# Two hand-ordered boundaries in a macaron decoder block: earlier transposes, a low half written by hand, and weight splits moved

## The chip, the core and the metric

The kernel runs on one core of a Trainium2 chip. The metric is the device time of one execution in microseconds. Engines are named TensorE (PE in the rows; PEld are its weight loads), VectorE (DVE), ScalarE (ACT), GpSimd (POOL) and SyncE (SP, which issues most transfers).

## The reference

One decoder block over 512 tokens of 1024 channels in float32: a SwiGLU feed-forward (width 2816), a token mixer and a second SwiGLU feed-forward, each between two RMS norms:

```python
f = swiglu(rms_norm(h, ffn1_pre_g), ffn1_w_gu, ffn1_w_down)
h = h + 0.5 * rms_norm(f, ffn1_post_g)
m = hybrid_mixer(rms_norm(h, mix_pre_g), ...)   # one input projection; RG-LRU and window attention; output projection
h = h + rms_norm(m, mix_post_g)
f = swiglu(rms_norm(h, ffn2_pre_g), ffn2_w_gu, ffn2_w_down)
h = h + 0.5 * rms_norm(f, ffn2_post_g)
```

## The kernel before

**Products.** Every float32 operand is split in two halves, a rounded one (`h`) and the rest (`l`), and a product is three matmuls (`mm3`, L166 to L169): high by high, high by low, low by high. The weights come in pieces of 128x1024, numbered in the order of use (`worder`): SP loads a piece (`wload`), ScalarE casts it to its high half (`wround`, L115), VectorE subtracts that from the piece (`wsplit`, L123) and issues the loads of the next three. `wget` takes the next piece and prepares two more ahead; `wnow` prepares none ahead. Pieces 50 to 53 are the mixer's first four x chunks, 54 and 55 its keys, 56 and 57 its values; 124 to 131 are the first gate and up chunks of the second feed-forward.

**The stages.** The first feed-forward's down product is a sum of seven products of blocks in Strassen's manner (order 1, 2, 3, 6, 5, 7, 4 in `down`); the token output projection (`token_out`) is the same in small. The last product, 4, is done for one of its two token tiles after the other: 33 matmuls each in `down` (six pieces, the last of half size), 12 in `token_out`.

**A boundary** between two stages handles four tiles of 128 tokens each (`boundary`). `half(t, i, z)` squares one half of a tile's columns on ScalarE with a sum (L515); `epilogue(t)` is a generator of five steps: (1) the sum and its power on GpSimd, and the gain (L519, L529, L212); (2) the residual sum in two halves on VectorE (L543), its squares on ScalarE (L548) and the store; (3) sum and power of these (L529, L212); (4) the normalised tile `un` in two halves (L556), which yields the number `FEATURE_LAG[name][t]`; (5) `to_features`: eight TensorE transposes (L227), the high half cast on ScalarE (L231), the low half on VectorE (L232), and in the second boundary copies of the raw values on ScalarE (L235). Tiles 0 and 1 are ready before the last product, 2 and 3 after its first and second pass. Boundary `b1` lies between the first feed-forward and the mixer, `b2` between the mixer and the second feed-forward, `b3` at the end.

**Ticks.** A generator that has yielded a number waits in the list `live`; each call of `tick()` lowers the number by one, and at zero the generator's next step is emitted there. In the last product of `down` there is a tick after each weight piece (six to a pass), in the feature chunks one after each chunk.

**Order.** Inside `with tc.manual_schedule()` each engine issues its instructions in the order in which they are written; the order across engines is left to semaphores. Outside of it a planner chooses the order with durations of its own, and it may put instructions written outside between those written inside. In the kernel before, `down` is inside to the end of its last product and of the epilogues that it starts; the mixer, from its first x chunk (`x_group`, `first_four`) on, is outside; `token_out` and the second feed-forward's gate and up stage are inside.

**The next stage's first chunks** need `u`, the transposed tiles: the low token half (tokens 0 to 255) needs tiles 0 and 1, the high half tiles 2 and 3. So the first four x chunks (`first_four`) and the first six chunks of the second feed-forward (`first_six`) are done for the low half first, 24 matmuls of 256 columns each, and then for the high half. The first chunk takes the low parts of `u` last (`low_last`).

Of the kernel before, what the change touches and what calls it, by code (L numbers as in the profile page):

```python
# [18 lines left out]
ATT_LAG = (3, 2)  # L19
WARM = 10  # L20
JSTD = {"f1": 6, "f2": 4}
FEATURE_LAG = {"b1": (7, 9, 7, 3), "b2": (1, 1, 5, 6)}
ATT_GATES = (2, 3, 4, 5, 6, 7)
T = 512
NT = T // P
# [16 lines left out]
def hybrid_block_kernel(ctx, tc, x, xt, g1, w_first, gains, gu1, gs1, dn1, w_x, w_gate, w_q, w_k, w_v, w_gl, w_ga, w_pl, w_pa,  # L42
# [85 lines left out]
    def wget():  # L128
        i = wpos[0]
        wpos[0] += 1  # L130
        wsplit(i + 1 + AHEAD)
        return wready[i]
# [101 lines left out]
                keep.append((raw[half][:, :, ts_], bv))  # L234
        return [lambda z=z, bv=bv: A.copy(z, bv) for z, bv in keep]  # L235

    def feat_chunk(b, w, u, tok, low_last=False):
        wh, wl = w
        if low_last:
            for n in range(2 * KD):  # L240
                k = n % KD
                ks = slice(k * P, (k + 1) * P)
                if n < KD:
                    PE.matmul(b[:, tok], lhsT=wh[:, ks], rhs=at(u, 0, k, tok), start=k == 0, stop=False)
                    PE.matmul(b[:, tok], lhsT=wl[:, ks], rhs=at(u, 0, k, tok), start=False, stop=False)
                else:
                    PE.matmul(b[:, tok], lhsT=wh[:, ks], rhs=at(u, 1, k, tok), start=False, stop=k == KD - 1)
            return
        for k in range(KD):
            ks = slice(k * P, (k + 1) * P)  # L250
            mm3(b[:, tok], wh[:, ks], wl[:, ks], at(u, 0, k, tok), at(u, 1, k, tok), k == 0, k == KD - 1)

    ALL = slice(0, T)
    HALVES = (slice(0, T // 2), slice(T // 2, T))

    def first_four(u, name, done):
        first = []
        for i in range(4):
            first.append((wget(), bank(f"{name}{i}")))
        for tok in HALVES:  # L260
            for i, (w, b) in enumerate(first):
                feat_chunk(b, w, u, tok, i == 0)
                tick()
                if tok is HALVES[1]:
                    done(i, b)

    def first_six(u, name, done, early):
        first = []
        for i in range(6):
            first.append((wnow(), bank(f"{name}{i}")))  # L270
            if i < 5:
                wsplit(wpos[0] + 1)
            feat_chunk(first[i][1], first[i][0], u, HALVES[0], i == 0)
            tick()
        for i, (w, b) in enumerate(first):
            if i == 2:
                early()
            if i >= 4:
                wsplit(wpos[0] + i - 3)
            feat_chunk(b, w, u, HALVES[1], i == 0)  # L280
            tick()
            done(i, b)

    def split_chunk(p, ph, pl, i):
        A.copy(ph[:, i, :], p[:, i, :])
# [206 lines left out]
    def boundary(src, dst, g_post, g_pre, u, scale, name, raw=None, then=None, unit=1.0):  # L492
        rhs = []

        def residual():
            t = len(rhs)
            if t < NT:
                rh = b8(f"{name}rh{t}", [P, 2, D])
                A.dma_start(rh[:, 0, :], src[t])
                rhs.append(rh)  # L500

        cols = (slice(0, 512), slice(512, 1024))
        sq, parts, late, copies = {}, {}, {}, []

        def half(t, i, z, sign=1.0, o=None, wait=False):
            if t not in sq:
                sq[t], parts[t], late[t] = sm(f"{name}ps{t}", 2), [None, None], []
                wait = wait or i == 1
            else:
                wait = True  # L510
            if o is None:
                while len(rhs) <= t:
                    residual()
                o = rhs[t][:, 1, cols[i]]
            A.activation(t4(f"{name}sq{t}{i}")[:, :512], z, AF.Square, scale=unit / 32.0, accum_out=sq[t][:, i:i + 1])  # L515
            parts[t][i] = o

            def gain():
                V.scalar_tensor_tensor(out=o, in0=z, scalar=sign * scale * unit, in1=g_post[:, cols[i]],  # L519
                                       op0=ALU.mult, op1=ALU.mult)  # L520

            if wait:
                late[t].append(gain)
            else:
                gain()

        def inverse(ms, z):
            me = sm(f"{name}{z}e")
            V.tensor_scalar(out=me, in0=ms[:, 0:1], scalar1=ms[:, 1:2], scalar2=EPS, op0=ALU.add, op1=ALU.add)  # L529
            return rstd(me, f"{name}{z}r")  # L530

        def epilogue(t):
            while len(rhs) < min(t + 2, NT):
                residual()
            res, h = rhs[t][:, 0, :], rhs[t][:, 1, :]
            r = inverse(sq[t], f"p{t}")
            for gain in late[t]:
                gain()
            yield
            if g_pre is not None:  # L540
                ms, un = sm(f"{name}ms{t}", 2), t4(f"{name}un{t}")
            for i in range(2):
                V.scalar_tensor_tensor(out=h[:, cols[i]], in0=parts[t][i], scalar=r, in1=res[:, cols[i]],  # L543
                                       op0=ALU.mult, op1=ALU.add)
                if g_pre is None:
                    (SP if i == 0 else A).dma_start(dst[t][:, cols[i]], h[:, cols[i]])
                else:
                    A.activation(un[:, cols[i]], h[:, cols[i]], AF.Square, scale=1.0 / 32.0, accum_out=ms[:, i:i + 1])  # L548
            if g_pre is None:
                return  # L550
            A.dma_start(dst[t], h)
            yield
            r = inverse(ms, f"n{t}")
            yield
            for i in range(2):
                V.scalar_tensor_tensor(out=un[:, cols[i]], in0=h[:, cols[i]], scalar=r, in1=g_pre[:, cols[i]],  # L556
                                       op0=ALU.mult, op1=ALU.mult)
            yield FEATURE_LAG[name][t]
            copies.extend(to_features(un, t, u, f"{name}n", raw))
            while t > 0 and copies:  # L560
                copies.pop(0)()
            if then is not None and t == NT - 1:
                start(then())

        return half, epilogue, residual

    def down(ps, name):
        lo_, hi_ = slice(0, 256), slice(256, 512)
# [86 lines left out]
            tick()  # L655

        piece(1, 0)
        half, epilogue, residual = yield
        with tc.manual_schedule():
            for i in (1, 2, 3, 6, 5, 7):  # L660
                for c in range(2 * (i == 1), KS if i < 7 else KS - 3, 2):
# [33 lines left out]
                    gens = []  # L695
                wsplit(wpos[0] + (KS + 1) // 2 - 1 + t)
            run(gens)
            ws = []
            for t in range(2):
                for c in range(0, KS, 2):  # L700
                    if t == 0:
                        ws.append(wget())
                    for cc in range(c, min(c + 2, KS)):
                        unit(4, cc, ws[c // 2], (t,))
                    tick()
                half(2 + t, 1, X[t], -1.0)
                start(epilogue(2 + t))
        yield

    def moving(raw, name, mv):  # L710
# [108 lines left out]
    g_post, g_pre = gain_pair(1, 2, "g_b1")  # L819
    u2 = new_u("u2")  # L820
    hs = [dram.tile([P, D], F32, name=f"h_spill{t}") for t in range(NT)]
    dn_run[0].send(boundary(xv, hs, g_post, g_pre, u2, 0.5, "b1"))

    vec = const.tile([P, 8, KD], F32, name="vec")
    sink = const.tile([P, NH], F32, name="sink")
# [79 lines left out]
    def x_group(gi):  # L905
        a4, m4, bx4 = (b8(f"{n}{gi}", [P, 4, T]) for n in ("la", "lm", "lb"))
        hl.append(m4)
        cr = range(4 * gi, 4 * gi + 4)
        if gi == 0:
            first_four(u2, "x", lambda c, b: start(lru_chunk(c, b, a4, m4, bx4, c == cr[-1])))  # L910
        else:
            for c in cr:
                w = wget()
                b = bank(f"x{c}")
                feat_chunk(b, w, u2, ALL)
                tick()
                start(lru_chunk(c, b, a4, m4, bx4, c == cr[-1]))
# [253 lines left out]
    def token_out():  # L1171
        X, Y, Q = ([bank(f"wo{z}{t}") for t in range(2)] for z in "XYQ")
        dst = {1: X, 2: Y, 6: X, 5: Q, 3: Q, 7: X, 4: X}
        half, epilogue, residual = boundary(hs, hs2, g_post, g_pre, u3, 1.0, "b2", raw3,
                                            lambda: moving(raw3, "u3", mv3), 0.5)

        def unit(i, k, w, tiles):
# [68 lines left out]
        w = [wnow() for _ in range(2)]  # L1246
        next(e[0])
        next(e[1])
        wsplit(wpos[0] + 1)
        next(e[0])  # L1250
        next(e[1])
        wround(wpos[0] + 4)
        for k in range(4):
            unit(4, k, w[k // 2], (0,))
        half(2, 0, X[0])
        for n in range(2):
            for k in (2 * n, 2 * n + 1):
                unit(4, k, w[n], (1,))
            if n == 1:
                half(3, 0, X[1])  # L1260
            next(e[n], None)
        wsplit(wpos[0] + 2)
        next(e[2])
        next(e[3])
        wsplit(wpos[0] + 3)
        next(e[2])
        next(e[3])
        wsplit(wpos[0] + 4)
        next(e[2])
        next(e[3])  # L1270
        wround(wpos[0] + 5)
        for t in (2, 3):
            live.append([e[t], next(e[t])])
            wsplit(wpos[0] + 5)

    dn_run = []
    with tc.manual_schedule():
        token_out()
        gate_up(u3, "f2", first_six, lambda: (gs2, blocks(u3, mv3)), begin(dn_run, "f2"), j0=3)
    g_post, _ = gain_pair(5, 1, "g_b3")  # L1280
    dn_run[0].send(boundary(hs2, ov, g_post, None, None, 0.5, "b3"))


_VECS = ["conv_b", "lru_b_a", "lru_b_x", "lru_lambda"]
# [94 lines left out]
```

## Time and profile before

| | |
|---|---|
| median of 3 runs | 1115.5 us (1113.28 to 1116.26) |
| profiled execution | 1116.43 us, of which the span (first to last instruction) is 1114.6 us |
| TensorE busy | 1100.9 us (99%), 6582 matmuls |
| VectorE busy | 901.2 us (81%) |
| ScalarE busy | 602.5 us (54%) |
| GpSimd busy | 85.0 us (8%) |
| TensorE's mean granted clock | 0.998 of full speed |

Busy time of TensorE counts a matmul from its start to its modelled end, and these overlap; how dense the matmuls stand is read from the distance of their starts. The span in 40 slices of 27.9 us shows 9 tenths or more for TensorE in all but the last.

### The profile page before, as it was taken

Reading aid. Unit: us, or ns where it says so; the run is one execution under the profiler, and the core shown is the slowest. Engines: PE = TensorE matmul, PEld = TensorE weight load, DVE = VectorE, ACT = ScalarE, POOL = GpSimd, SP = SyncE. Lnnn points to the kernel's source line nnn. Section 1 sums busy time; section 2 is a strip of 40 time slices with the busy share of each in tenths; the row PEclk is TensorE's granted clock in tenths of the full one; section 3 lists DMA queues with packets and bytes.
Section 4 is the critical chain, followed back from the end, with each engine's and each line's share of the span. In section 5 each row is a group of like instructions: output and inputs, shape, how many; then the busy total and the mean of one; then the engine's idle time right before and its main releaser. Section 6 shows DMA issues by size and latency. Waiting matters only on the chain. (4 is left out here: it accounts for less than half of the span.)

```text
span 1114.6 us, 16931 instructions
## 1 busy us (share of the span) xinstructions
PE 1100.9 (99%) x6582; PEld 981.9 (88%) x6582; DVE 901.2 (81%) x1357; ACT 602.5 (54%) x1003; POOL 85.0 (8%) x90
## 2 busy tenths in 40 slices
PE   9999999999999999999999999999999999999997
PEld 7889999988878888888888888888999999998885
DVE  6998998889898798988767461579689888988896
ACT  7435544465664658576555442257445455456662
POOL 1000010000000001123112200001000000000000
PEclk9999999999999999999999999999999999999999
DMA  9239999664677172712822791446339999455483
GB/s 362 75 128 251 305 299 283 210 229 123 211 263 274 65 207 73 211 42 73 264 77 88 261 279 53 134 167 230 123 112 289 305 277 303 125 168 191 151 267 121
DMA packets 55295, 213.60 MB, mean 192 GB/s; under 512 B 6576, under 2 KB 6704, under 8 KB 49456
## 3 DMA queue, kind: packets, MB, share of 16 engines
q1 hardware_dynamic: 46288, 166.92, 44.1%
q0 software_dynamic: 4608, 31.46, 13.4%
q10 hardware_dynamic: 4320, 14.16, 3.5%
q8 instruction: 51, 0.84, 0.3%
q14 instruction: 28, 0.23, 0.1%
HBM read 200.98 MB, written 66.06 MB: 240 GB/s over the span
## 5 line engine op out<-in xcount | busy, mean ns | idle before, releaser
L123 DVE TENSOR_TENSOR w<-wraw,w 128x1024 fp32r<-128x1024 f32 x174 | 204.3, 1193 | 24.6 <-ACT w L115 24.2
L115 ACT CAST w<-wraw 128x1024 fp32r<-128x1024 f32 x174 | 169.0, 1012 | 31.4 <-PE glp L169 8.3
L169 PE MATMUL f1X<-u1m,f1W 128*128 128x256 f32 x256 | 72.5, 283 | 0.1
L168 PE MATMUL f1X<-u1m,f1W 128*128 128x256 f32 x256 | 72.4, 283 | 0.0
L167 PE MATMUL f1X<-u1m,f1W 128*128 128x256 f32 x256 | 72.4, 283 | 0.0
L169 PEld LDWEIGHTS f1X<-u1m,f1W 128*128 128x128 f32 x256 | 49.1, 192 | 0.3 <-DVE f1W L371 0.3
L167 PEld LDWEIGHTS f1X<-u1m,f1W 128*128 128x128 f32 x256 | 49.1, 192 | 0.1
L168 PEld LDWEIGHTS f1X<-u1m,f1W 128*128 128x128 f32 x256 | 49.1, 192 | 0.1
L1152 DVE SCALAR_TENSOR_TENSOR gas<-gas,gap 128x512 f32<-128x512 f32 x8 | 5.5, 688 | 45.2 <-PE gap L169 45.2
L169 PE MATMUL f2X<-u3m,f2W 128*128 128x256 f32 x144 | 40.9, 284 | 0.1
L168 PE MATMUL f2X<-u3l,f2W 128*128 128x256 f32 x144 | 40.8, 283 | 0.0
L169 PE MATMUL f2X<-u3h,f2W 128*128 128x256 f32 x144 | 40.8, 283 | 0.0
L167 PE MATMUL f2Q<-u3m,f2W 128*128 128x256 f32 x144 | 40.8, 283 | 0.0
L168 PE MATMUL f2Q<-u3m,f2W 128*128 128x256 f32 x144 | 40.8, 283 | 0.0
L169 PE MATMUL f2Q<-u3m,f2W 128*128 128x256 f32 x144 | 40.8, 283 | 0.0
L167 PE MATMUL f2X<-u3m,f2W 128*128 128x256 f32 x144 | 40.8, 283 | 0.0
L168 PE MATMUL f2X<-u3m,f2W 128*128 128x256 f32 x144 | 40.7, 283 | 0.0
L167 PE MATMUL f2X<-u3h,f2W 128*128 128x256 f32 x144 | 40.7, 283 | 0.0
L167 PE MATMUL f1Q<-u1m,f1W 128*128 128x256 f32 x128 | 36.2, 283 | 0.0
L168 PE MATMUL f1Q<-u1m,f1W 128*128 128x256 f32 x128 | 36.2, 283 | 0.0
L169 PE MATMUL f1Q<-u1m,f1W 128*128 128x256 f32 x128 | 36.2, 283 | 0.0
L168 PE MATMUL f2X<-w,f2y 128*128 128x512 f32 x88 | 34.5, 392 | 0.4 <-DVE w L123 0.4
(880 smaller groups left out, 3796.9 us busy)
## 6 DMA issues: line engine op xcount, KB each, us to landing
wraw<-wsum SPq DMA_DIRECT2D x40, 512.0 KB, 4.3
wsum<-in_dn_dram SPq DMA_DIRECT2D x16, 1024.0 KB, 10.5
wraw<-in_dn_dram SPq DMA_DIRECT2D x30, 512.0 KB, 4.7
f2L<-in_gs_dram SPq DMA_DIRECT2D x18, 512.0 KB, 5.1
f2R<-in_gs_dram SPq DMA_DIRECT2D x18, 512.0 KB, 5.1
wraw<-in_gu_dram SPq DMA_DIRECT2D x16, 512.0 KB, 6.5
f1L<-in_gs_dram SPq DMA_DIRECT2D x16, 512.0 KB, 5.2
f1R<-in_gs_dram SPq DMA_DIRECT2D x16, 512.0 KB, 5.4
```

The costliest lines, as they stand in the source:

```text
L115: A.copy(w[:, 0, :], raws[n])
L123: V.tensor_tensor(out=w[:, 1, :], in0=raws[n], in1=w[:, 0, :].bitcast(F32), op=ALU.subtract)
L167: PE.matmul(o, lhsT=ah, rhs=bh, start=start, stop=False, skip_group_check=reopen)
L168: PE.matmul(o, lhsT=ah, rhs=bl, start=False, stop=False, skip_group_check=reopen)
L169: PE.matmul(o, lhsT=al, rhs=bh, start=False, stop=stop, skip_group_check=reopen)
L1152: V.scalar_tensor_tensor(out=s, in0=s, scalar=1.0, in1=b, op0=ALU.add, op1=ALU.mult)
```

## The change

Five edits. (1) `FEATURE_LAG` of `b1` goes from (7, 9, 7, 3) to (5, 6, 2, 4). (2) `first_four` goes; its low half is `low_half`, emitted by hand from within `down`'s last product (`by_hand`), and its high half `high_half`, emitted where `first_four` was. `low_half` takes its pieces with `wnow` and a split one ahead, and has its last tick inside the last chunk, three of its eight weight blocks before the end. (3) The epilogues of tiles 2 and 3 in `b1` are stepped by hand, with casts and splits of pieces 52 and 53 between their steps. (4) The raw copies of tile 1 no longer follow its transposes at once; `flush` emits them. (5) In `token_out` the square of the last tile and the copies go behind tile 1's transposes, and the splits of pieces 124 to 129 move among the steps of the epilogues. `first_six` is now `low_half` and `high_half` as well.

```diff
-FEATURE_LAG = {"b1": (7, 9, 7, 3), "b2": (1, 1, 5, 6)}
+FEATURE_LAG = {"b1": (5, 6, 2, 4), "b2": (1, 1, 5, 6)}
...
-    def feat_chunk(b, w, u, tok, low_last=False):
+    def feat_chunk(b, w, u, tok, low_last=False, within=None):
...
         for k in range(KD):
+            if k == KD - 3 and within is not None:
+                within()
             ks = slice(k * P, (k + 1) * P)
...
-    def first_four(u, name, done):
+    def low_half(u, name, n):
         first = []
-        for i in range(4):
-            first.append((wget(), bank(f"{name}{i}")))
-        for tok in HALVES:
-            for i, (w, b) in enumerate(first):
-                feat_chunk(b, w, u, tok, i == 0)
+        for i in range(n):
+            first.append((wnow(), bank(f"{name}{i}")))
+            if i < n - 1:
+                wsplit(wpos[0] + 1)
+            feat_chunk(first[i][1], first[i][0], u, HALVES[0], i == 0, tick if i == n - 1 else None)
+            if i < n - 1:
                 tick()
-                if tok is HALVES[1]:
-                    done(i, b)
+        return first
+
+    def high_half(u, first, done, between=lambda i: None):
+        for i, (w, b) in enumerate(first):
+            between(i)
+            feat_chunk(b, w, u, HALVES[1], i == 0)
+            tick()
+            done(i, b)
 
     def first_six(u, name, done, early):
-        first = []
-        for i in range(6):
-            first.append((wnow(), bank(f"{name}{i}")))
-            if i < 5:
-                wsplit(wpos[0] + 1)
-            feat_chunk(first[i][1], first[i][0], u, HALVES[0], i == 0)
-            tick()
-        for i, (w, b) in enumerate(first):
+        def between(i):
             if i == 2:
                 early()
             if i >= 4:
                 wsplit(wpos[0] + i - 3)
-            feat_chunk(b, w, u, HALVES[1], i == 0)
-            tick()
-            done(i, b)
+
+        high_half(u, low_half(u, name, 6), done, between)
...
+        def flush():
+            while copies:
+                copies.pop(0)()
...
             copies.extend(to_features(un, t, u, f"{name}n", raw))
-            while t > 0 and copies:
-                copies.pop(0)()
+            if t > 1:
+                flush()
...
                 half(2 + t, 1, X[t], -1.0)
-                start(epilogue(2 + t))
+                if not by_hand:
+                    start(epilogue(2 + t))
+                    continue
+                e.append(epilogue(2 + t))
+                if t == 0:
+                    next(e[0])
+                    next(e[0])
+                    wround(wpos[0] + 4)
+                    continue
+                next(e[0])
+                next(e[1])
+                next(e[1])
+                wsplit(wpos[0] + 3)
+                lags = [next(e[0])]
+                next(e[1])
+                lags.append(next(e[1]))
+                wsplit(wpos[0] + 4)
+                live.extend([x, n] for x, n in zip(e, lags))
+                by_hand()
...
-    dn_run[0].send(boundary(xv, hs, g_post, g_pre, u2, 0.5, "b1"))
+    x_low = []
+    dn_run[0].send((boundary(xv, hs, g_post, g_pre, u2, 0.5, "b1"), lambda: x_low.extend(low_half(u2, "x", 4))))
...
-            first_four(u2, "x", lambda c, b: start(lru_chunk(c, b, a4, m4, bx4, c == cr[-1])))
+            high_half(u2, x_low, lambda c, b: start(lru_chunk(c, b, a4, m4, bx4, c == cr[-1])))
...
         next(e[0])
         next(e[1])
-        wsplit(wpos[0] + 1)
         next(e[0])
         next(e[1])
+        wsplit(wpos[0] + 1)
         wround(wpos[0] + 4)
...
-            if n == 1:
-                half(3, 0, X[1])
             next(e[n], None)
+        half(3, 0, X[1])
+        flush()
         wsplit(wpos[0] + 2)
         next(e[2])
         next(e[3])
         wsplit(wpos[0] + 3)
+        wround(wpos[0] + 4)
         next(e[2])
-        next(e[3])
         wsplit(wpos[0] + 4)
-        next(e[2])
         next(e[3])
         wround(wpos[0] + 5)
+        next(e[2])
+        wsplit(wpos[0] + 5)
+        next(e[3])
         for t in (2, 3):
             live.append([e[t], next(e[t])])
-            wsplit(wpos[0] + 5)
```

## Rows read from the trace of the kernel before

**Rows 1.** The page: the span and the line of busy times.
```profile
span 1114.6 us, 16931 instructions
PE 1100.9 (99%) x6582; PEld 981.9 (88%) x6582; DVE 901.2 (81%) x1357; ACT 602.5 (54%) x1003; POOL 85.0 (8%) x90
```
**Rows 2.** Who TensorE waited for: us in total, times, longest.
```profile
PE b1ntp L227 <- DVE b1un L556: 1.8, 1, 1.8
...
PE f2f L169 <- DVE w L123: 0.9, 2, 0.6
PE at10b L998 <- DMA qt<-q_halves: 0.8, 1, 0.8
```
**Rows 3.** Timeline, TensorE, first boundary: start, length, instruction, [idle before <- releaser].
```profile
331.46 0.39 PE L169 MATMUL f1X<-w,f1y 128*128 128x512 f32 x1
331.69 0.40 PE L167 MATMUL f1X<-w,f1y 128*128 128x512 f32 x1
332.36 0.50 PE L168 MATMUL f1X<-w,f1y 128*128 128x512 f32 x1 [0.27 <-DVE w L123]
...
334.31 1.03 PE L227 MATMUL b1ntp<-ident,b1un 128*128 128x128 f32 x8
...
342.64 0.39 PE L244 MATMUL x<-u2h,w 128*128 128x256 f32 x1 [0.25 <-ACT u2h L231]
...
352.00 0.28 PE L168 MATMUL x<-u2l,w 128*128 128x256 f32 x1
352.12 0.28 PE L169 MATMUL x<-u2h,w 128*128 128x256 f32 x1
354.19 1.29 PE L227 MATMUL b1ntp<-ident,b1un 128*128 128x128 f32 x8 [1.78 <-DVE b1un L556]
...
355.97 0.41 PE L169 MATMUL x<-u2h,w 128*128 128x256 f32 x1
...
359.17 0.31 PE L169 MATMUL x<-u2h,w 128*128 128x256 f32 x1
...
359.67 0.28 PE L244 MATMUL x<-u2h,w 128*128 128x256 f32 x1
```
**Rows 4.** Windows: stretch, length, busy us of five engines, PEclk, DMA share, GB/s.
```profile
356.00:358.00 2.00, 2.00 (x11) 2.00 (x11) 1.75 (x3) 2.00 (x4) 0.00 (x0) 0.50 0.56 172
```
**Rows 5.** Timeline, VectorE, first boundary.
```profile
333.09 1.42 DVE L556 SCALAR_TENSOR_TENSOR b1un<-b1rh,b1n0r,g_b 128x512 f32<-128x512 f32 x2 [0.37 <-POOL b1n0r L212]
...
338.02 0.21 DVE L529 TENSOR_SCALAR b1p2e<-b1ps 128x1 f32<-128x1 f32 x1
...
338.95 0.75 DVE L543 SCALAR_TENSOR_TENSOR b1rh<-f1a,b1p2r,b1rh 128x512 f32<-128x512 f32 x1
...
346.50 2.35 DVE L123 TENSOR_TENSOR w<-wraw,w 128x1024 fp32r<-128x1024 f32 x2
```
**Rows 6.** Timeline, ScalarE, first boundary.
```profile
342.94 0.64 ACT L515 ACTIVATE b1sq<-f1X 128x512 f32<-128x512 f32 x1
...
343.52 2.97 ACT L115 CAST w<-wraw 128x1024 fp32r<-128x1024 f32 x3
```
**Rows 7.** Timeline, TensorE, second boundary.
```profile
766.43 1.32 PE L227 MATMUL b2ntp<-ident,b2un 128*128 128x128 f32 x8
...
770.44 0.39 PE L244 MATMUL f2f<-u3h,w 128*128 128x256 f32 x1 [0.44 <-ACT u3h L231]
...
780.46 0.38 PE L169 MATMUL f2f<-u3h,w 128*128 128x256 f32 x1 [0.65 <-DVE w L123]
...
783.86 0.39 PE L169 MATMUL f2f<-u3h,w 128*128 128x256 f32 x1 [0.28 <-DVE w L123]
...
791.62 0.39 PE L244 MATMUL f2f<-u3h,w 128*128 128x256 f32 x1 [0.24 <-ACT u3h L231]
```
**Rows 8.** Timelines, VectorE and ScalarE, second boundary.
```profile
764.49 1.22 DVE L123 TENSOR_TENSOR w<-wraw,w 128x1024 fp32r<-128x1024 f32 x1
...
779.93 1.98 ACT L115 CAST w<-wraw 128x1024 fp32r<-128x1024 f32 x2
```

More of the change, by code (lines that the diff above doesn't have):

```diff
@@ L559, in epilogue @@
             copies.extend(to_features(un, t, u, f"{name}n", raw))
-            while t > 0 and copies:
-                copies.pop(0)()
+            if t > 1:
+                flush()
             if then is not None and t == NT - 1:
                 start(then())
-        return half, epilogue, residual
+        return half, epilogue, residual, flush
     def down(ps, name):
@@ L657, in down @@
         piece(1, 0)
-        half, epilogue, residual = yield
+        (half, epilogue, residual, _), by_hand = yield
         with tc.manual_schedule():
@@ L697, in down @@
             run(gens)
-            ws = []
+            ws, e = [], []
             for t in range(2):
@@ L1173, in token_out @@
         dst = {1: X, 2: Y, 6: X, 5: Q, 3: Q, 7: X, 4: X}
-        half, epilogue, residual = boundary(hs, hs2, g_post, g_pre, u3, 1.0, "b2", raw3,
+        half, epilogue, residual, flush = boundary(hs, hs2, g_post, g_pre, u3, 1.0, "b2", raw3,
                                             lambda: moving(raw3, "u3", mv3), 0.5)
@@ L1280, in hybrid_block_kernel @@
     g_post, _ = gain_pair(5, 1, "g_b3")
-    dn_run[0].send(boundary(hs2, ov, g_post, None, None, 0.5, "b3"))
+    dn_run[0].send((boundary(hs2, ov, g_post, None, None, 0.5, "b3"), None))
 _VECS = ["conv_b", "lru_b_a", "lru_b_x", "lru_lambda"]
```

## The prediction, made before the result was known

> **What bounds the kernel now.** I read the page first, then who TensorE waited for, then TensorE's timeline around the two places the change touches, and VectorE's and ScalarE's beside it. The page says that TensorE is busy in 1100.9 of 1114.6 us [rows 1]: what can be won is the time between its matmuls, and only where it stands. The reader is to see in the view of waits that nearly all named waits lie at the two token-tile boundaries: 1.8 us for the normalised tile (`b1un`) at the first, 0.9 us for weight halves in the first chunks of the second feed-forward, `f2f` [rows 2]. Taking the spacing of TensorE's starts, 0.23 us for a 512-column matmul and 0.12 us for a 256-column one [rows 3], whatever lies above that between 316 and 375 us adds up to some 4.9 us, and between 755 and 830 us to 4.4 us. That is all these two edits can touch.
>
> The largest piece is at the first boundary. [...] Fifteen steps between the starts at 355.97 and 359.17 take 3.20 us where 15 x 0.12 = 1.80 would do [rows 3]: the fall costs 1.4 us on top of the wait.
>
> **First boundary, part one: the transposes of tiles 0 and 1.** Their lag goes from 7 and 9 ticks to 5 and 6. A tick is one weight piece of the last product's pass over one tile: 6 matmuls, the sixth 3. So before, tile 0 is transposed six matmuls into the second pass; after, behind matmul 30 of the first pass's 33. In the trace matmul 30 starts at 331.46, so the transposes come up at 331.69, where matmul 31 started before [rows 3]. Nothing that VectorE does before that is changed, so its pair for tile 0 still starts at 333.09 and takes 1.42 [rows 5]: first half written at 333.84, second at 334.50. I choose to believe this: TensorE takes its instructions in the written order, and it now waits 331.69 to 333.88, 2.2 us, and 0.27 more for the second half. The wait for the sixth piece's low half in that place (331.69 to 332.36 where 0.23 would do, 0.44, and 0.10 at the restart [rows 3]) is covered by it. Eight transposes hold TensorE 0.8 us as before (the row at 334.31 is 1.03 long, of which the last 0.2 runs under the next matmul). Then three matmuls (0.68), tile 1's transposes (ready at 335.87, no wait), restart 0.08, and 33 x 0.227 = 7.48: the second pass ends at 344.06, where before the next stage began at 342.64 [rows 3]. This part loses 1.4 us.
>
> **First boundary, part two: the four x chunks' low token half, tiles 2 and 3.** Before, from 342.64 to the first high half at 359.67 [rows 3] it took 17.0 us. The work in it is 96 matmuls of 0.12 = 11.5 us and two times 0.8 us of transposes, 13.1 us. After, tile 2's transposes stand behind chunk 1, at 344.06 + 48 x 0.12 = 349.8, and tile 3's behind matmul 15 of chunk 3. Are the tiles ready? ScalarE first casts two weights by hand (0.99 each [rows 6]) behind tile 2's squares, which end at 343.4: free at 345.3. The square of the last product's tile takes 0.64 and its read 0.19 [rows 6], so VectorE's sum comes at 346.1. From there to the residual product it is 0.93 (338.02 to 338.95 for tile 2 [rows 5]), two of these 1.33, the split of w52 1.14: tile 2's normalised halves are there at 350.2 and 350.85. TensorE waits 0.4 and 0.27 us. Tile 3's are ready at 353.0, and its transposes are due at 356: three us to spare, and the 1.95 us wait goes. What is late next is tile 2. High half: 344.06 + 13.1 + 0.67 + 0.25 for restarts = 358.1, against 359.67. **Both parts: 1.6 us saved**, of which all but 0.2 is the fall of the clock.
>
> The four weight splits that leave the planner's stretch cost nothing there: the next weights (54 to 56) are first multiplied some 12 us later, and VectorE has about 5 us free behind tile 3's chain. If that cover is gone it is 1.14 us each. Where the planner puts them no row of before can show. Before, it put two splits of together 2.35 us just ahead of tile 3's residual products [rows 5]. So: from 0 (they fall into the 2.4 us in which VectorE waits for the square) to 2.3 us more in tile 2's wait. I take 0 for the forecast, the end whose idle time I can name, and keep 2.3.
>
> **Second boundary.** The split of w124 goes behind tiles 0 and 1's normalisation: these start at 764.95 instead of 765.62, since 764.49 plus 1.22 was the split [rows 8]. Tile 0's transposes, due at 766.19, no longer wait for halves (766.43 and 1.32 long before [rows 7], 0.24 + 0.28). The square of the last tile and the four raw copies go behind tile 1's casts on ScalarE, so these start at 769.05 instead of 769.81, and the first chunk at 769.65 instead of 770.44 [rows 7]: 0.8 us saved. w124's split ends at 768.8, in time for the second matmul.
>
> Then VectorE's order changes: split 126, tile 2's residuals, split 127, tile 3's residuals, split 128, both normalisations, split 129. Against the chunks' low halves of 2.87 us each: chunk 2 (775.4) waits for split 126 until 776.2, 0.57 us, some 0.3 more than before; chunk 3 no longer waits, which before cost 0.91 (780.46); chunk 4 waits 1.1 against 0.54 (783.86 [rows 7]). For w128 it is ScalarE that is late: the cast stands behind tile 3's squares, as before at 779.93 [rows 8], done at 781.8, so VectorE idles 1.8 us and the split ends at 783.0. Chunk 5 waits 0.2. Tile 3's transposes now stand inside chunk 5, nine matmuls (1.1 us) before its end, which covers the cast that the high half waited for at 791.62 [rows 7], 0.6 us. The high half starts at 790.6. **1.0 us saved.** Bounds: 1.6 saved if split 128 finds its weight cast (no wait in chunk 4 beyond 0.5), 0 if split 126 and 128 are each half a microsecond later than worked out.
>
> The last feed-forward's end has no hand-written low half behind it; it stays. The `flush` and the moved prefetch loads on SP put nothing new in front of a load that TensorE waits for: rows 2 name one wait on a transfer, 0.8 us for the queries, 110 us after the first boundary.
>
> **Sum.** The profiled execution took 1116.43 us, its span 1114.6 and 1.8 around it. 1116.43 - 1.6 - 1.0 = 1113.8. The median of the runs, 1115.5, lies 0.9 below that execution (1113.28 to 1116.26). The runs differ by 3.0 us, twice the fall's price, so some of them may not have the fall; against such a run this change wins 1.2, not 2.6.
>
> **Rivals.** (a) The clock falls in the new place. TensorE stands still 2.2 us and then only transposes and three matmuls come before 336.6; that is at least the pause before the fall of rows 4. For it: 2.2 against 1.8 us. Against it: the stretch is broken differently. Price 1.4: 1115.2.
> [...]
>
> (b) The other side: the planner fills VectorE's hand-ordered gaps with the splits of weights 54 and 55 (and their casts on ScalarE) ahead of tile 3's residuals, as it did before [rows 5]. Then tile 2's normalisation is 2.3 us later, TensorE waits 2.9 us there, and the clock falls after it: 1113.8 + 2.3 + 1.4 = 1117.5, slower than before. It decides from 1.3 us of filling on, with the fall, or 2.6 without. Against it: VectorE has those 2.4 us of idle time ahead of the chain.
>
> (c) The gain is larger: the fall is gone, tile 2's 0.67 us wait too (if the pow and the square run at their shortest), and the planner's new order drops the wait for the queries with its restart, 1.0 us [rows 2]: 1113.8 - 1.7 = 1112.1, or 1111.2 counted from the median.
>
> (d) The change does not do what it says: with lag 5 the transposes would be held back to where the tile is ready. An order by hand can't do that.
>
> **Chances.** Forecast 0.42; (a) 0.27; (b) 0.11; (c) 0.20; (d) nothing. The measurement can tell about 0.3%, 3.3 us: faster is below 1112.15, slower above 1118.85. Faster is (c) for the most part and a tail of the forecast, 0.24; slower the upper half of (b) and a re-planned mixer stretch that I can't work out, 0.08; same 0.68. The range goes from (c) counted from the median to (b): 1111.0 to 1117.3.
>
> **What would show it.** Right: in the changed trace TensorE idles about 2.2 us ahead of tile 0's transposes at 331.7 to 333.9, released by VectorE's `b1un`; no wait of 1.8 us at tile 3; tile 2's wait 0.4 to 0.7; the high half starts near 358.1; in the second boundary a wait of some 1.1 us for split 128 and none for split 127. Wrong: no wait at 331.7 (then VectorE's order there is not what I read), a fall of the clock near 334 to 338, splits of the mixer's key weights between tile 3's sum and its residuals, or a high half of the second feed-forward no earlier against its first chunk.

## The result, and the profile after

The changed kernel takes 1119.5 us (median of 6 runs, 1118.57 to 1119.96); the kernel before took 1115.47 beside it (6 runs). The ratio is 1.0038, 95% interval 1.0025 to 1.0051: it is slower, where 1113.8 was predicted, and above the range. The profiled execution took 1118.8 us, its span 1117.0, 2.4 more than before [rows 1].

The page of the kernel after, span and busy times:

```profile
span 1117.0 us, 16935 instructions
...
PE 1100.5 (99%) x6582; PEld 982.0 (88%) x6582; DVE 899.0 (80%) x1357; ACT 603.5 (54%) x1003; POOL 84.4 (8%) x90
```

The busy times differ by 2.2 us at most, the work is the same; so the time must lie between the matmuls. Who TensorE waited for, of the kernel after (us in total, times, longest):

```profile
PE kk L167 <- ACT w L115: 4.0, 1, 4.0
PE b1ntp L227 <- DVE b1un L561: 2.0, 1, 2.0
...
PE f2f L169 <- DVE w L123: 0.9, 2, 0.7
PE kk L169 <- DVE w L123: 0.5, 1, 0.5
...
PE at10b L1022 <- DMA qt<-q_halves: 0.3, 1, 0.3
```

Against [rows 2] the wait for `b1un` stands as predicted, 2.0 us. The first line is new: the mixer's keys (`kk`, pieces 54 and 55) wait 4.0 us for a cast on ScalarE, and 0.5 for a split. The prediction has no such wait. TensorE's timeline after, at the first boundary and at the keys:

```profile
332.80 1.77 PE L227 MATMUL b1ntp<-ident,b1un 128*128 128x128 f32 x8 [2.02 <-DVE b1un L561]
334.23 0.77 PE L167 MATMUL f1X<-w,f1y 128*128 128x512 f32 x1
...
335.65 1.44 PE L227 MATMUL b1ntp<-ident,b1un 128*128 128x128 f32 x8
336.85 0.48 PE L167 MATMUL f1X<-w,f1y 128*128 128x512 f32 x1
...
357.68 0.28 PE L244 MATMUL x<-u2h,w 128*128 128x256 f32 x1
...
371.84 0.40 PE L169 MATMUL i<-xch,bd 128*128 128x512 f32 x1
376.20 0.50 PE L167 MATMUL kk<-u2h,w 128*128 128x512 f32 x1 [3.96 <-ACT w L115]
376.54 0.40 PE L168 MATMUL kk<-u2l,w 128*128 128x512 f32 x1
377.46 0.80 PE L169 MATMUL kk<-u2h,w 128*128 128x512 f32 x1 [0.52 <-DVE w L123]
378.05 0.63 PE L167 MATMUL kk<-u2h,w 128*128 128x512 f32 x1
378.48 0.63 PE L168 MATMUL kk<-u2l,w 128*128 128x512 f32 x1
```

Windows of the kernel after (columns as in [rows 4]; the granted clock is the third number from the end):

```profile
331.00:334.00 3.00, 1.20 (x7) 1.05 (x8) 2.55 (x7) 1.56 (x4) 1.06 (x2) 0.84 1.02 416
334.00:337.00 3.00, 3.00 (x15) 2.60 (x14) 3.00 (x6) 2.17 (x4) 0.00 (x0) 0.59 0.30 123
...
378.00:379.00 1.00, 1.00 (x4) 0.76 (x3) 1.00 (x2) 1.00 (x3) 0.00 (x0) 0.50 0.46 66
```

The reader is to see two falls of the granted clock: behind the wait at tile 0 (0.59 of full speed in the mean of three microseconds) and behind the waits at the keys (0.50 in the row shown). A 128x512 matmul that otherwise starts 0.23 us after the last starts 0.43 after it between 378 and 380.6.

Up to the first boundary's work both executions do the same, and the one after happened to be 1.09 us ahead when it got there. In all thirteen profiled executions of this document that matmul (331.46 in [rows 3]) starts between 329.87 and 331.46, so an offset of this size comes by chance. With it taken off, the balance is:

| stretch | change, us | how read |
|---|---|---|
| start of the execution | -1.1 | distance of the same matmuls ahead of the boundary |
| first boundary to the high half | -0.9 | 357.68 + 1.09 against 359.67 [rows 3] |
| at the keys | +6.6 | waits 3.96 + 0.52, restarts 0.45, slow steps 1.66 |
| wait for the queries | -0.5 | 0.8 [rows 2] to 0.3 |
| second boundary | -1.7 | -1.2 to the high half, -0.56 a wait and its restart 18 us behind it that are gone |
| sum | +2.4 | 1117.0 - 1114.6 |

Why the keys wait stands in ScalarE's timeline of the kernel after:

```profile
357.32 1.06 ACT L899 CAST bd<-bdraw 128x1024 fp32r<-128x1024 f32 x1
362.68 0.78 ACT L889 ACTIVATE xc<-x,vec 128x512 f32<-128x512 f32 x1 [4.29 <-PE x L247]
...
373.87 0.82 ACT L913 ACTIVATE tr<-tr,nsp 128x512 f32<-128x512 f32 x1
374.58 0.64 ACT L914 ACTIVATE lm<-la 128x512 f32<-128x512 f32 x1
375.10 3.89 ACT L115 CAST w<-wraw 128x1024 fp32r<-128x1024 f32 x4
```

The casts of pieces 54 to 57 stand in a row behind the gate work of chunk 0 (L908 to L914), though ScalarE stood idle 4.29 us ahead of 362.68. In the kernel before the cast of 54 was one of the three at 343.52 [rows 6], the cast of 55 followed at 355.99, and `kk` began at 373.02 without a wait.

### The profile page after: what moved, and what is told of

Same layout as the page of the kernel before. It is cut to its first block, busy times and chain, and to the rows that moved or that the text cites. A ratio compares the mean times of both kernels' runs of the same rounds, so it can differ in the third digit from the quotient of the medians.

```text
span 1117.0 us, 16935 instructions
## 1 busy us (share of the span) xinstructions
PE 1100.5 (99%) x6582; PEld 982.0 (88%) x6582; DVE 899.0 (80%) x1357; ACT 603.5 (54%) x1003; POOL 84.4 (8%) x90
```

## The experiments

Each ran in alternation with the kernel before; its time stands beside that one's median in the same series.

**1. The key weights written earlier, left to the planner.** In `x_group`:

```diff
+            wsplit(wpos[0] + 2)
             high_half(u2, x_low, ...)
```

> The changed kernel, but with the cast and split of the keys' weights (54 and 55) written ahead of the x chunks' high half, outside the hand-ordered region. Theory 1, they are late in the order: TensorE's waits of 3.96 and 0.52 us at the first key matmuls go, and with them the restart and the fall of the clock behind them, 6.9 us by the spacing of the starts; the planner may put one cast ahead of tile 3's square, up to 0.7 us back: 1112.6 to 1113.3. Theory 2, ScalarE and VectorE are full with the recurrent gates there and the wait only moves: 1118 or more, with TensorE waiting for the gates' operands or the key weights a little later.

Measured: 1115.5 (10 runs, 1115.12 to 1116.91) against 1115.65; ratio 1.0004 (0.9994 to 1.0013). Neither theory's number. The wait at the keys is gone, 4 us against the changed kernel, but splits now stand where the prediction's rival (b) has them. VectorE's timeline in this kernel:

```profile
344.78 1.22 DVE L123 TENSOR_TENSOR w<-wraw,w 128x1024 fp32r<-128x1024 f32 x1 [2.62 <-ACT w L115]
345.93 0.20 DVE L530 TENSOR_SCALAR b1p3e<-b1ps 128x1 f32<-128x1 f32 x1
...
349.32 1.41 DVE L561 SCALAR_TENSOR_TENSOR b1un<-b1rh,b1n2r,g_b 128x512 f32<-128x512 f32 x2
350.65 0.21 DVE L530 TENSOR_SCALAR b1n3e<-b1ms 128x1 f32<-128x1 f32 x1
350.77 1.22 DVE L123 TENSOR_TENSOR w<-wraw,w 128x1024 fp32r<-128x1024 f32 x1
```

The planner put one split ahead of tile 3's sum and one between the two normalisations. Tile 2's transposes then waited 0.5 us, the fourth x chunk 0.4 for a split, and the gates of a later chunk 1.3 for a cast on ScalarE. TensorE's row at tile 2:

```profile
350.22 1.29 PE L227 MATMUL b1ntp<-ident,b1un 128*128 128x128 f32 x8 [0.49 <-DVE b1un L561]
```

**2. The key weights written by hand, behind the low halves.**

```diff
-    ..., lambda: x_low.extend(low_half(u2, "x", 4))))
+    ..., lambda: (x_low.extend(low_half(u2, "x", 4)), wsplit(wpos[0] + 2))))
```

> As the run before, but the two casts and splits are written by hand at the end of the low half, behind tile 3's casts and low parts. Theory 1: 1112.6, and tile 2's and 3's chains as in the changed kernel. Theory 2: 1118 or more.

Measured: 1113.15 (10 runs, 1112.22 to 1113.84) against 1115.65; ratio 0.9985 (0.9975 to 0.9994). ScalarE's timeline in this kernel shows the two casts where it was idle:

```profile
357.91 2.01 ACT L115 CAST w<-wraw 128x1024 fp32r<-128x1024 f32 x2
359.81 1.06 ACT L899 CAST bd<-bdraw 128x1024 fp32r<-128x1024 f32 x1
```

No wait is left at the keys. With one call moved, the changed kernel is some 6 us faster and beats the kernel before: nearly all of the 6.6 of the balance.

**3. and 4. Each boundary alone.** The first is the change without its edits to the second boundary (`token_out`, the early tick in the first six chunks, the raw copies), the second is the kernel before with these edits only.

> The changed kernel with the second boundary as it was before. If the two boundaries add up: the changed kernel plus 1.1 (second boundary) and 0.6 (the wait at the first full-width chunk of the second feed-forward): 1121.2. If the second boundary's edits do nothing: 1119.5.

> The kernel before with the second boundary of the changed one. If they add up: 1115.5 - 1.1 - 0.6 = 1113.8. If the second boundary's edits do nothing: 1115.5.

Measured: first boundary alone 1120.95 (4 runs, ratio 1.006, 1.0042 to 1.0078), second alone 1113.34 (10 runs, 0.9983, 0.9972 to 0.9994), both against 1115.65. By the medians +5.3 and -2.3 make +3.0, where both together measured +4.0; that is within the intervals, so the two add as far as these runs can tell. The whole loss comes from the first boundary's edits, and the second's win about what the balance gives.

**5. and 6. The written place, one chunk apart.** The two splits are written in the done-step of the four x chunks, behind the second (`c == 1`) or the third (`c == 2`) chunk's high half, and left to the planner:

```diff
-            high_half(u2, x_low, lambda c, b: start(lru_chunk(...)))
+            high_half(u2, x_low, lambda c, b: (start(lru_chunk(...)), c == 1 and wsplit(wpos[0] + 2)))
```

> The changed kernel, with the splits of the two key weights written behind the second chunk's high half and left to the planner. Theory 1 (the 4.0 us wait at the keys comes from where the two casts are first written: up to the tick that emits the gates' second step they are placed ahead of it): casts near 358 us, no wait of TensorE at kk, no fall of the clock at 376 to 381, about 1113.2 as in the run by hand. Rival (the early place was won only by the order by hand, or by being written ahead of the whole high half): casts behind the gates, wait of 3.5 to 4 us at kk, about 1119.5.

> The same two splits written one chunk later, behind the third chunk's high half, which is behind the tick that emits the gates' second step. Theory 1: casts again in a row behind the gate steps of chunk 0 (near 375 us), wait of about 4 us at kk and the second fall of the clock: about 1119.5, as the changed kernel itself, though all that is different from the run before is one place in the written order. Rival (the planner places a cast where ScalarE is idle, and only the distance to the use counts): casts at 358 to 363 us where ScalarE is idle, no wait, about 1113.

Measured against 1115.8: behind the second chunk 1113.08 (10 runs, 0.9982, 0.9972 to 0.9991), behind the third 1118.92 (4 runs, 1.0039, 1.0024 to 1.0054). ScalarE's timelines, first of the fifth kernel, then of the sixth:

```profile
358.51 1.06 ACT L899 CAST bd<-bdraw 128x1024 fp32r<-128x1024 f32 x1
359.46 2.00 ACT L115 CAST w<-wraw 128x1024 fp32r<-128x1024 f32 x2
```

```profile
374.69 0.64 ACT L914 ACTIVATE lm<-la 128x512 f32<-128x512 f32 x1
375.20 3.89 ACT L115 CAST w<-wraw 128x1024 fp32r<-128x1024 f32 x4
```

Both theory 1's numbers, to 0.6 us. What lies between the two written places is the third chunk's high half with its tick, which emits the second step of chunk 0's gates, and the first step of the third chunk's gates; experiment 9 tells these apart. A cast written ahead of that second step is placed where ScalarE is idle; written behind it, it is placed behind it.

**7. and 8. Without the early transposes.** From the kernel of experiment 2: lags back to 7 and 9, casts of 52 and 53 ahead of tile 2's residuals, tile 2's normalisation ahead of tile 3's sum; the eighth also has the cast of 128 earlier.

```diff
-FEATURE_LAG = {"b1": (5, 6, 2, 4), ...
+FEATURE_LAG = {"b1": (7, 9, 2, 4), ...
...
                 if t == 0:
+                    wround(wpos[0] + 4)
                     next(e[0])
                     next(e[0])
-                    wround(wpos[0] + 4)
                     continue
                 next(e[0])
-                next(e[1])
-                next(e[1])
                 wsplit(wpos[0] + 3)
                 lags = [next(e[0])]
                 next(e[1])
+                next(e[1])
+                wsplit(wpos[0] + 4)
+                next(e[1])
                 lags.append(next(e[1]))
-                wsplit(wpos[0] + 4)
```

```diff
+        wround(wpos[0] + 5)
         wsplit(wpos[0] + 4)
         next(e[3])
-        wround(wpos[0] + 5)
```

> The changed kernel with the key weights by hand, the lags of tiles 0 and 1 back at 7 and 9, and the hand order of the last two tiles so changed that tile 2 does not wait for tile 3's sum: casts of weights 52 and 53 ahead of tile 2's residuals, split of 52 and tile 2's normalisation ahead of tile 3's sum, split of 53 behind tile 3's residuals. Theory 1 (all that the early lag does is to make a wait of 2.04 us at tile 0 and the fall of the clock behind it, 1.99 us): both go, 0.5 us come back at the sixth piece's low half (0.44 and 0.10), no wait at tile 2 (normalised about 346.8, due 348.4) nor tile 3 (352.1, due 353.5): 1113.15 - 3.5 = 1109.7. Rival (some wait is needed anyway, since VectorE's chain to tile 3 sets the time): the wait comes up again at tile 2 or 3, 1112 to 1113.

> The kernel of the run before with, at the second boundary, the cast of weight 128 ahead of tile 3's residuals and their squares. Theory (the 0.9 us wait of chunk 4 comes from ScalarE, whose cast of 128 stands behind tile 3's squares, so VectorE idles 1.6 us for it): the wait and its restart of 0.1 go, tile 3's squares are 1.0 later, still ahead of its transposes: 1.0 less than the run before, 1108.7. Rival (the split of 128 is held by VectorE's own queue, splits 126 and 127 and the residuals): no change, 1109.7.

Measured against 1115.8: 1111.38 (6 runs, 1111.32 to 1111.61, ratio 0.9967, 0.9955 to 0.9978) and 1110.38 (4 runs, 0.9959, 0.9945 to 0.9974). The eighth wins the expected 1.0 over the seventh. The seventh is 1.7 above its expectation; its view of waits shows why:

```profile
PE r L167 <- ACT xch L894: 1.3, 1, 1.3
...
PE f2f L169 <- DVE w L123: 0.9, 2, 0.7
...
PE x L244 <- ACT u2h L231: 0.2, 1, 0.2
```

The waits at the four tiles are gone as expected, and a new one of 1.3 us (1.5 with its restart) stands at the gates at 369.11, where the planner put a cast (`xch`) behind an activation that reads a gate's result. In the eighth the 0.7 at piece 128 is gone. VectorE's split of it now finds its cast:

```profile
776.72 0.20 DVE L530 TENSOR_SCALAR b2n2e<-b2ms 128x1 f32<-128x1 f32 x1
776.85 1.21 DVE L123 TENSOR_TENSOR w<-wraw,w 128x1024 fp32r<-128x1024 f32 x1
```

**9. The gates' second step written later.** The changed kernel with

```diff
-LRU_LAG = (2, 2)
+LRU_LAG = (4, 2)
```

> The changed kernel as it is (key weights left to the planner, first written at the keys), with the lag of the recurrent gates' first step at 4 ticks instead of 2, so that the second step of chunk 0 is written behind the keys' first weights. Theory 1 (a cast is held behind the gates' second step because that step is written ahead of it): the casts of 54 and 55 come ahead of the gate steps, near 358 to 362 us, and the 4.0 us wait and the clock's second fall go: 1113 to 1114, although nothing at the weights is edited. Rival (the casts are late because they are written behind the four x chunks): wait of about 4 us at kk as before, about 1119.

Measured: 1119.62 (4 runs, ratio 1.0042, 1.0027 to 1.0057) against 1115.23. The time is the rival's, the mechanism theory 1's. ScalarE's timeline, the view of waits, and two of TensorE's rows at `gt`, a product of the mixer some 90 us later:

```profile
358.50 2.95 ACT L115 CAST w<-wraw 128x1024 fp32r<-128x1024 f32 x3
```

```profile
PE gt L169 <- DVE w L123: 2.1, 2, 1.5
PE b1ntp L227 <- DVE b1un L561: 2.0, 1, 2.0
...
PE gt L167 <- ACT w L115: 1.1, 1, 1.1
...
PE v L168 <- DVE w L123: 0.7, 1, 0.7
PE q L167 <- DVE gp L1074: 0.6, 1, 0.6
```

```profile
461.66 0.50 PE L169 MATMUL gt<-u2h,w 128*128 128x512 f32 x1 [1.54 <-DVE w L123]
...
468.01 0.50 PE L167 MATMUL gt<-u2h,w 128*128 128x512 f32 x1 [1.07 <-ACT w L115]
```

The casts of 54 to 56 moved to 358.5 with no edit at the weights, and the 4.0 us wait is gone. But the lag holds for all of the first four chunks, and waits for weights came up later, 3.2 us at `gt` and 0.7 at `v`; behind the last of them the clock falls again, to 0.58 in the mean of four microseconds, so that the new waits cost about what the old ones did:

```profile
470.00:474.00 4.00, 4.00 (x12) 3.10 (x12) 3.27 (x5) 2.83 (x6) 1.04 (x1) 0.58 0.67 176
```

The first steps of the third and fourth chunk's gates are written ahead of the casts here too, and do not hold them. So it is the written order against that step that places the cast; the constant is not a way to use it.

**10. The late lags alone.** The kernel of experiment 2 with `FEATURE_LAG` (7, 9, 2, 4) for `b1` and nothing else.

> The changed kernel with the key weights by hand, and of the rest the lags of tiles 0 and 1 alone back at 7 and 9. Theory 1 (the early lag makes the 2.04 us wait and the fall, but the hand order needs it, since the casts of 52 and 53 stand ahead of the four u2 casts of tiles 0 and 1 on ScalarE): no wait at tile 0; the first x matmul waits some 1 to 2 us for u2, tile 2 waits again as its normalisation stands behind tile 3's sum (about 1 us), and a fall of the clock may follow either: 1112 to 1114, no better than 1113.15. Rival (the lags are all there is to it): no new wait, 1109.9.

Measured: 1112.99 (10 runs, 1111.91 to 1114.28, ratio 0.9987, 0.9977 to 0.9996) against 1115.23: no better than experiment 2, as theory 1 has it. Its first wait, and ScalarE's rows behind it:

```profile
PE x L244 <- ACT u2h L231: 2.1, 1, 2.1
```

```profile
339.69 1.98 ACT L115 CAST w<-wraw 128x1024 fp32r<-128x1024 f32 x2
341.57 2.03 ACT L231 CAST u2h<-b1ntp 128x512 fp32r<-128x512 f32 x4
```

The casts of 52 and 53 stand ahead of the four casts that the first x chunk needs. The wait of about 2 us moves from tile 0 to that chunk unless the two casts move as well, as they do in experiment 7; tile 2's transposes lost 0.5 us where 1 was expected.

**11. Only the casts of the key weights by hand.** Experiment 8 with `wround(wpos[0] + 2)` in place of the `wsplit` in the lambda.

> The fastest kernel so far (1110.38), with only the casts of the two key weights by hand and their splits left to the planner. The trace of that kernel has one wait left in the stretch, 1.28 us and 0.27 of restart at the gates of chunk 1, for a cast on ScalarE that the planner put behind the activation that reads the first gate's result; the compiled order of this kernel has that cast ahead of it. Theory: wait gone, 1108.9. Rival (chunk 1's convolution is late on VectorE itself): the wait stays, 1110.4.

Measured: 1108.77 (4 runs, 1108.39 to 1109.16) against 1115.23; ratio 0.9947 (0.993 to 0.9963). The wait at the gates is gone, and none is left at the keys though their splits are the planner's again: it is the cast that has to be early. This is the fastest version, 10.7 us below the changed kernel's median and 6.5 below the kernel before.

## Why the prediction was wrong

**The step that failed** is "The four weight splits that leave the planner's stretch cost nothing there". Its cover, 12 us to the first use and 5 us free on VectorE, was there; it was the wrong cover. The piece was late on ScalarE, by its cast, because of the order: `first_four` took its pieces with `wget`, which writes the next two casts ahead of its high halves; `low_half` takes them with `wnow`, so these casts are first written at the keys, behind the gates of chunk 0. That is in the diff. The prediction priced a late split at 1.14 us each; what it cost was 4.48 us of waits, 0.45 of restarts and 1.66 of lower clock, 6.6 in all. Experiments 2 and 5 take it away, 6 brings it back with one written place, and 9 takes it away by moving the gates' step alone. Why the planner keeps to that order though ScalarE is idle is open: it may be that it hands out buffers in the written order. That was not tried by itself.

**First boundary.** Part one was right to a tenth: 2.0 us of wait at tile 0 for 2.2 predicted, released by `b1un`. The clock fell behind it, as rival (a) has it, at 1.8 us instead of 1.4: the two sets of transposes and three matmuls between 332.80 and 336.85 took 4.05 us where 2 x 0.79 + 0.68 = 2.26 would do. Since TensorE came later by that, tile 2's wait of 0.67 did not occur, and the high half began 0.9 us earlier, not 1.6. So the new wait costs 3.8 us, more than the wait and fall that it replaced (1.95 for the wait that ends at 354.19 and 1.4 for the slow steps behind it [rows 3], where the granted clock was 0.50 of full speed [rows 4]). The forecast's sum has no fall in the new place; it stands only in the rival. The prediction takes from the spread of the runs that some of them may not have the old fall: for the old place the runs agree, in the new one all seven profiled executions show a fall (last section).

**Rival (b)** gave the same sign by another way. In the changed kernel the splits of 54 and 55 were late, not early. Experiment 1 has them where the rival puts them, but tile 2 then waits 0.5 us, not 2.9, and the clock does not fall there: the matmuls of 256 columns behind it start 0.12 us apart. Experiment 1 is 2.4 us behind experiment 2, and most of that stands elsewhere: 1.3 us at the gates and 0.4 at the fourth x chunk.

**Second boundary.** 1.2 us saved to the high half for 1.0 predicted. By the distance of the starts above 0.12 us, chunk 2 waits 0.37 (0.57 predicted), chunk 3 not at all, chunk 4 0.9 (1.1). TensorE after, the two that answer to [rows 7]:

```profile
780.42 0.38 PE L169 MATMUL f2f<-u3h,w 128*128 128x256 f32 x1 [0.21 <-DVE w L123]
...
787.17 0.39 PE L169 MATMUL f2f<-u3h,w 128*128 128x256 f32 x1 [0.74 <-DVE w L123]
```

That chunk 4's wait is ScalarE's cast of 128 was right; experiment 8 takes it away for 1.0 us. A wait for a split 18 us later, 0.56 us with its restart, which the prediction's sum had not touched, went as well.

**The wait for the queries** fell from 0.8 to 0.3 us here. In the other kernels it lies between 0.2 and 1.3, and in experiments 3 and 9 there is none: it changes with where the rest stands, and no sum of the prediction needed it.

## What to carry to other kernels

When a helper that prepares ahead is replaced by one that doesn't, list every piece that it used to prepare beyond its own, for each engine and queue that prepares it, and find where each is now first written: the first use tells when it is needed, the written place when it may come. When work is taken from a planner into an order by hand, the work that stays behind is planned anew, and its waits must be looked for tens of microseconds later. A wait of TensorE of 2 us cost nearly twice its length here where the clock fell behind it (3.8 us at tile 0), so moving a wait wins nothing by itself: price it in its new place, with the fall.

## What the runs showed of the hardware

In these runs the clock fell behind some of TensorE's waits of about 2 us and not behind others, and, by the mean clock of the runs, behind the same wait in some executions and not in others. Seven profiled executions have the wait of 2.0 us at tile 0: the changed kernel and experiments 1, 2, 3, 5, 6 and 9. In all seven the two sets of transposes and three matmuls behind it take 1.6 to 2.0 us more than their 2.26. The granted clock between 334 and 337 was 0.59 of full speed in the changed kernel, 0.50 in experiment 2, 0.67 in 5 and 0.53 in 9. The window of experiment 2, the wait ending at 333.18:

```profile
334.00:337.00 3.00, 3.00 (x12) 2.61 (x13) 3.00 (x5) 1.99 (x3) 0.00 (x0) 0.50 0.45 182
```

In experiment 10 TensorE waits 2.1 us within ten microseconds of the same place, and in the profiled execution the granted clock behind it stays at full speed (1.00). The wait ends at 343.17:

```profile
343.00:346.00 3.00, 2.83 (x23) 2.83 (x24) 2.54 (x7) 1.19 (x4) 1.07 (x2) 1.00 0.35 76
```

The work behind the two waits differs: transposes at tile 0, matmuls of 256 columns here. Whether that decides was not tried.

The mean granted clock of each run says more. In experiment 4, which keeps the old wait of 1.8 us at tile 3, four runs of 1111.3 to 1112.4 us have 0.999 and six of 1112.8 to 1114.7 have 0.997; the profiled one, with the fall (matmuls of 256 columns 0.21 us apart behind the wait), is of the six. In experiment 10 four runs of 1111.9 to 1112.5 have 0.998 or 0.999 and six of 1113.0 to 1114.3 have 0.997; the profiled one, without a fall, is of the four. So by the mean clock the executions of these two kernels fall into some with a fall and some without, whose median times lie 2.4 and 1.5 us apart. The kernel before, with the same wait as experiment 4, agrees by its times, though its clocks overlap: 25 runs of one series fall into 9 between 1113.2 and 1114.1 and 16 between 1115.3 and 1117.1, with none between. Experiments 2 and 5, with the wait at tile 0, show no such groups: of their 20 runs 16 have 0.997 and none is above 0.998. That fits a fall there in every execution but does not prove it, as experiment 8, without such a wait, has 0.998 as well.
